# Moving the experts' gathers, the combination's split and the fold's product in a fused two-model kernel

## The chip, the cores and the metric

One core of a Trainium2 chip runs the whole program in one launch. The metric is device time in microseconds, the median of several executions. The engines are PE (TensorE: products, PEld its weight loads), DVE (VectorE), ACT (ScalarE), POOL (GpSimd) and SP (SyncE, which here only issues transfers).

## The reference, cut to what matters

Two small transformer stacks run one behind the other on 256 tokens of width 1024, in float32. The change lies in one stage, the second layer's feed-forward part with eight experts, of which each token uses two:

```python
def moe_swiglu(h, router_w, router_b, w1, w3, w2):      # h: 256 x 1024, w1 and w3: 8 x 1024 x 3584, w2: 8 x 3584 x 1024
    logits = (hf @ router_w) + router_b
    top_logit, top_idx = lax.top_k(logits, 2)
    top_w = jax.nn.softmax(top_logit, axis=-1)
    ...                                                  # rows of each expert in groups
    def expert_block(args):
        toks, e = args
        xb = h_pad[toks]
        return (jax.nn.silu(xb @ w1[e]) * (xb @ w3[e])) @ w2[e]
    ...
    y = y * row_w[:, None]
    out = jax.ops.segment_sum(y, row_tok, num_segments=T + 1)[:T]
```

So each expert takes the tokens that chose it (the gather), multiplies them by W1 and W3, then by W2, and its rows go back, weighted, to their tokens (the combination).

## The kernel before, in words

**Split products.** Each float32 operand is split into a high part in the type fp32r (a cast on ACT) and a low part (what is left, a subtraction on DVE), and a product is the sum of two or three products of parts. All weights are split so on their way: SP loads 1 MiB into a buffer `raw` (eight buffers in the experts' stage), ACT casts 1024 columns at a time into `whi`, DVE subtracts into `wlo`, and PE uses both.

**Places.** The eight experts are worked off in places 0 to 7, sorted by the number of their tokens. Even places hold up to 128 tokens. Odd places hold up to 64, and the 64 rows of the high part and the 64 of the low part lie side by side in one operand of 128 columns. So an even place needs three products for each block of weights and an odd one two, and then the two halves of the odd result have to be added: `folded` (line 1937) copies the bank `h` from PSUM to the buffer `hc` on ACT and multiplies it in plain float32 by a fixed matrix `fold` on PE, back into the same bank. There are 14 folds in an odd place: W1 and W3 of seven blocks of 512 columns.

**A place** has an up part (lines 2025 to 2050: seven blocks b, in each 8 x 512 columns of W1 and of W3) and a down part (lines 2053 to 2066: 28 steps of W2 into two banks `py`). In an odd place these are 224 and 112 products of 512 columns, in an even one 336 and 168.

**Chains.** Everything beside these products is written as Python generators. A list of chains is kept; behind each product of an odd place, and behind every first or second of an even one, `gap()` lets each chain go on to its next `yield`. A chain's step is held back while a rough model of the engines' times (`Meter`, `Flow`) says that its operands aren't ready. So the number of `yield`s sets how many products lie between two steps in PE's queue. The splits of the next weights are emitted between them by the same model. The chains that matter:

- `gather(e)` (line 1881), with `slots` (line 1812): compares positions to make a 0/1 matrix `oh` (DVE); for each half of the columns four products pick the rows (bank `m`), ACT scales them into `xt`, PE transposes, ACT adds a shift and casts the high part, DVE subtracts for the low part; at its end come `ct` and `ws` for the combination. It is started at the beginning of the down part of place e - 1 (line 2051) and has to be through before place e starts (line 2019). Even places use the first 128 columns of `src.hh` and `src.hl`, odd ones columns 128 to 256 of `src.hh`.
- `combine(e)` (line 1967): for each half, ACT scales `py` into `ys`, ACT casts it into `yh`, DVE subtracts into `yl`; then 16 products of `yh` and `yl` with `ct`, and DVE adds the result into `x`. It is started behind the place's last product, so that it runs in the next place's up part; for place 7 it is emitted at once.
- `hidden` and `hidden64` (lines 1919 and 1945): Silu, the product, transposes and the split of the inner activations; `hidden64` runs the fold first and waits for both.

Of the kernel before, what the change touches and what calls it, by code (L numbers as in the profile page):

```python
# [10 lines left out]
F32 = mybir.dt.float32  # L11
F32R = mybir.dt.float32r
I32 = mybir.dt.int32
AF = mybir.ActivationFunctionType
OP = mybir.AluOpType
PSUM = bass.MemoryType.PSUM

P = 128
T = 256
# [51 lines left out]
def shape_constants():  # L71

    i = np.arange(P)
    base, mix, moe, nsa = Pack(), Pack(), Pack(), Pack()
    base.add("ident", np.eye(P))
    base.add("ones", np.ones((P, P)))
# [312 lines left out]
class Kern:  # L389
# [1383 lines left out]
    def moe(self, src, sh, g, aim):  # L1773

        nc, tc = self.nc, self.tc
        from contextlib import ExitStack
        F = 3584
        with ExitStack() as es:
            pp = es.enter_context(tc.tile_pool(name="moe", bufs=2))
# [29 lines left out]
            X, C = {}, {}  # L1809
# [39 lines left out]
            def slots0(oh, xh, xl):  # L1849

                cs = pp.tile([P, 1], F32, name="cs")
                pc = self.nbank()
                ps = [psh.tile([P, 512], F32, name=f"h{q}") for q in range(2)]
                for q in range(2):
                    n = 0
                    for s in (th, tl):
                        for i in range(2):
                            nc.tensor.matmul(ps[q], oh[:, i], s[:, i, q * 512:(q + 1) * 512], start=(n == 0), stop=(n == 3))
                            n += 1
                    for i in range(2 if q == 0 else 0):  # L1860
                        nc.tensor.matmul(pc[:, :1], oh[:, i].bitcast(F32), src.y[:, i:i + 1], start=(i == 0), stop=(i == 1))
                nc.scalar.copy(cs, pc[:, :1])
                ts = [pp.tile([P, 512], F32, name=n, bufs=1) for n in ("xt", "ys")]
                pt = [psh.tile([P, 512], F32, name=f"h{q}") for q in range(2)]
                nc.scalar.mul(ts[0], ps[0], cs)
                nc.vector.tensor_scalar(ts[1], ps[1], cs, None, op0=OP.mult)
                for q in range(2):
                    for j in range(4):
                        nc.tensor.transpose(pt[q][:, j * P:(j + 1) * P], ts[q][:, j * P:(j + 1) * P], self.ident)
                ts = [t.rearrange("p (k s) -> p k s", k=4) for t in ts]  # L1870
                for q in range(2):
                    c = slice(4 * q, 4 * q + 4)
                    nc.vector.tensor_tensor(ts[q], pt[q].rearrange("p (k s) -> p k s", k=4),
                                            sh[:, c, None].to_broadcast([P, 4, P]), op=OP.add)
                    nc.scalar.copy(xh[:, c], ts[q])
                for q in range(2):
                    c = slice(4 * q, 4 * q + 4)
                    nc.vector.tensor_tensor(xl[:, c], ts[q], xh[:, c].bitcast(F32), op=OP.subtract)
                yield

            def gather(e):

                oh = pp.tile([P, 2, P], F32R, name="oh")
                while e and "wP" not in r:
                    yield
                pos = r["posP" if e else "pos"]
                for i in range(2):
                    nc.vector.tensor_scalar(oh[:, i], self.C("iota64" if e % 2 else "iota"), pos[:, i, e:e + 1], None,
                                            op0=OP.is_equal)
                for _ in range(9 if e else 1):  # L1890
                    yield
                if e % 2:
                    xh, xl = src.hh[:, :, P:P + 64], src.hh[:, :, P + 64:T]
                else:
                    xh, xl = src.hh[:, :, :P], src.hl[:, :, :P]
                if e == 0:
                    yield from slots0(oh, xh, xl)
                else:
                    yield from slots(e, oh, xh, xl)
                    yield  # L1900
                X[e] = (src.hh[:, :, P:T], None) if e % 2 else (xh, xl)
                if e == 0:
                    yield
                    while "w" not in r:
                        yield
                pt = misc()
                for i in range(2):
                    nc.tensor.transpose(pt[:, i * P:(i + 1) * P], oh[:, i].bitcast(F32), self.ident)
                for i in range(2):
                    nc.tensor.matmul(pt[:, 256:257], oh[:, i].bitcast(F32), r["wP" if e else "w"][:, i, e:e + 1],  # L1910
                                     start=(i == 0), stop=(i == 1))
                yield
                ct = pp.tile([P, T], F32R, name="ct")
                nc.scalar.copy(ct, pt[:, :T])
                ws = pp.tile([P, 1], F32, name="ws")
                nc.vector.tensor_copy(ws, pt[:, 256:257])
                C[e] = (ct, ws)

# [17 lines left out]

            def folded(h, done):

                c = pp.tile([P, 512], F32, name="hc", bufs=1)
                nc.scalar.copy(c, h)  # L1940
                yield
                nc.tensor.matmul(h[:64], self.C("fold"), c, start=True, stop=True)
                done.append(h)

# [22 lines left out]
            def combine(e, py, last):  # L1967
                ct, ws = C[e]
                yh = pp.tile([P, D], F32R, name="yh", bufs=1)
                yl = pp.tile([P, D], F32R, name="yl", bufs=1)  # L1970
                pts = []

                def spread(q):
                    pt = psh.tile([P, 512], F32, name=f"h{q % 2}") if last else misc()
                    for j in range(2):
                        kc = 2 * q + j
                        o = pt[:, j * T:(j + 1) * T]
                        nc.tensor.matmul(o, yh[:, kc * P:(kc + 1) * P], ct, start=True, stop=False)
                        nc.tensor.matmul(o, yl[:, kc * P:(kc + 1) * P], ct, start=False, stop=True)
                    pts.append(pt)  # L1980

                for q in range(2):
                    s = slice(q * 512, (q + 1) * 512)
                    y = pp.tile([P, 512], F32, name="ys", bufs=1)
                    nc.scalar.mul(y, py[q], ws)
                    yield
                    nc.scalar.copy(yh[:, s], y)
                    yield
                    nc.vector.tensor_tensor(yl[:, s], y, yh[:, s].bitcast(F32), op=OP.subtract)
                    yield  # L1990
                    if last:
                        spread(2 * q)
                        spread(2 * q + 1)
                for _ in range(1 if last else 9):
                    yield
                for q in range(4):
                    if not last:
                        spread(q)
                        yield
                    for j in range(2):  # L2000
                        kc = 2 * q + j
                        nc.vector.scalar_tensor_tensor(self.x[:, kc], pts[q][:, j * T:(j + 1) * T], g[:, kc:kc + 1],
                                                       self.x[:, kc], op0=OP.mult, op1=OP.add)
                        if last:
                            self.x_done(kc)
                    for _ in range(1 if last else 9):
                        yield

            gap = self.idle
            self.refill()  # L2010
            for b in self.ahead:
# [4 lines left out]
                next(first)  # L2016
            self.chain(first)
            for e in range(8):
                while any(c[2] == ("g", e) for c in self.chains):
                    self.rest()  # L2020
                xh, xl = X[e]
                few = e % 2 == 1
# [2 lines left out]
                for b in range(F // 512):  # L2025
                    hs, done = [], []
                    for w in range(2):
                        ps = psh.tile([P, 512], F32, name=f"h{w}")
                        k = 0
                        while k < KC:  # L2030
                            _, k0, nk, hi, lo = self.block()
                            assert k0 == k
                            for j in range(nk):
                                c = slice(j * 512, (j + 1) * 512)
# [13 lines left out]
                    else:  # L2048
                        self.wait_for(lambda n, ps, hs=hs, b=b: self.chain(hidden(hs[0], hs[1], b, ah, al)),
                                      b, None, always)  # L2050
                if e < 7:
                    self.chain(gather(e + 1), ("g", e + 1))
                py = [psy.tile([P, 512], F32, name="lin") for q in range(2)]
                for k in range(F // P):
                    _, k0, nk, hi, lo = self.block()
# [3 lines left out]
                    for q in range(2):  # L2059
                        c = slice(q * 512, (q + 1) * 512)  # L2060
# [14 lines left out]
                if e == 0:  # L2075
# [2 lines left out]
                    over = nc.values_load(r["over"][:1], min_val=0, max_val=1)  # L2078
                    with tc.If(over > 0):  # L2079
                        self.moe_rest(src, sh, r, th, tl, g, pp, p1, psh, misc)  # L2080
                self.chain(combine(e, py, False))
            self.extra = self.nbank = None

    def route(self, src, pool, misc):
# [1216 lines left out]
```

## Time and profile before

| | us |
|---|---|
| median of 3 runs | 3192.83 (3192.02 to 3202.15) |
| profiled execution | 3196.97 |
| its span | 3195.2 |
| PE busy in the span | 3040.6 (95%) |
| DVE busy | 2550.7 (80%) |
| ACT busy | 2029.0 (64%) |

The profile comes from one execution. It has a page with totals, a list of waits (who stood idle until whom), a chain of waits that leads back from the last instruction, a timeline, and windows, which give each engine's busy time in stretches that one chooses, with the mean clock that PE was granted (1.00 is 2.4 GHz), the busy share of the 16 transfer engines and their rate. A matmul's row is longer than the time to the next one, since they are pipelined: in a dense run of 512 columns a new one starts each 0.23 us and each row says about 0.40. All computing instructions bear the same line, that of a helper (L315), and are told apart by tile: `h` are the banks of the up part, `lin` those of the down part, `m` those of gather, transposes and combination.

### The profile page before, as it was taken

What the parts mean: (1) busy time and instruction counts of PE and PEld (TensorE: products, weight loads), DVE (VectorE), ACT (ScalarE), POOL (GpSimd) and SP (SyncE); (2) the same over time, 40 slices, a digit from 0 to 9 for tenths busy, and PEclk for the clock granted to TensorE, in tenths of its full rate; (3) what the DMA queues carried; (4) which work ended last, traced back from release to release, by engine and by line L of the source; (5) the groups of instructions that cost most, each with busy time, mean ns of one, the idle gap of its engine ahead of it and who ended that gap; (6) DMA issues with size and microseconds to landing.
All of it is one profiled execution on the core that took longest, in us unless ns stands there. A gap on an engine that the chain in (4) does not pass through costs nothing.

```text
span 3195.2 us, 55851 instructions
## 1 busy us (share of the span) xinstructions
PE 3040.6 (95%) x20747; PEld 2717.3 (85%) x20747; DVE 2550.7 (80%) x4692; ACT 2029.0 (64%) x3928; POOL 168.7 (5%) x551
## 2 busy tenths in 40 slices
PE   5999999999999998999999999999899999999999
PEld 5999999999999885686686686699888999998999
DVE  7787789867767888998998998898896666767775
ACT  5565555456665687887887877855675544555554
POOL 2322000003320000000000000000000000000000
PEclk9999999999999999999999999999999999999999
DMA  7334568842234798998999998744305554551354
GB/s 258 118 136 159 189 223 294 290 160 88 98 106 161 279 356 326 379 354 332 380 356 341 370 367 330 303 172 169 123 28 197 170 201 157 174 185 41 118 182 150
DMA packets 155354, 704.56 MB, mean 221 GB/s; under 512 B 15280, under 2 KB 19264, under 8 KB 111296
## 3 DMA queue, kind: packets, MB, share of 16 engines
q1 hardware_dynamic: 154176, 698.25, 60.4%
q8 instruction: 165, 2.70, 0.3%
q10 hardware_dynamic: 896, 2.65, 0.2%
q14 instruction: 117, 0.96, 0.1%
HBM read 699.76 MB, written 1.07 MB: 219 GB/s over the span
## 4 chain that ended last, share of the span: by engine, by line
PE 47%; ACT 6%; DVE 5%; issue 3%; DMA 1%; POOL 0%; ACTq 0%; SPq 0%; DVEq 0%; POOLq 0%
PE lin L315 29%; PE h L315 11%; ACT whi L315 3%; DVE wlo L315 2%; PE m L315 1%; PE o L315 1%; ACT hc L315 1%; PE b L315 1%; DVE wt L315 1%; PE c L315 1%; DVE w L315 1%; PE cmph L315 0%; PE a L315 0%; DVE s5Es L315 0%; PE more L315 0%
## 5 line engine op out<-in xcount | busy, mean ns | idle before, releaser
L315 ACT CAST whi<-raw 128x512 fp32r<-128x512 f32 (+4 forms) x1852 | 1329.2, 752 | 648.7 <-PE lin L315 328.7
L315 DVE TENSOR_TENSOR wlo<-raw,whi 128x512 fp32r<-128x512 f32 (+4 forms) x1852 | 1531.3, 856 | 244.2 <-ACT whi L315 226.0
L315 PE MATMUL lin<-hh,whi 128*128 128x256 f32 (+2 forms) x2968 | 866.8, 292 | 11.7 <-ACT whi L315 5.0
L315 PE MATMUL lin<-hh,wlo 128*128 128x256 f32 (+2 forms) x2968 | 855.3, 288 | 5.2 <-DVE wlo L315 5.1
L315 PE MATMUL lin<-hl,whi 128*128 128x256 f32 (+2 forms) x2968 | 852.7, 287 | 5.7 <-DVE hl L315 5.7
L315 PEld LDWEIGHTS lin<-hh,whi 128*128 128x128 f32 (+1 forms) x2968 | 566.9, 191 | 21.9 <-issue 5.8
L315 PEld LDWEIGHTS lin<-hh,wlo 128*128 128x128 f32 (+1 forms) x2968 | 566.6, 191 | 12.1 <-DVE wlo L315 7.5
L315 PEld LDWEIGHTS lin<-hl,whi 128*128 128x128 f32 (+1 forms) x2968 | 565.7, 191 | 8.8 <-DVE hl L315 6.6
L315 PE MATMUL h<-whi,hh 128*128 128x512 f32 x896 | 363.5, 406 | 6.1 <-PEq L2079 4.2
L315 PE MATMUL h<-wlo,hh 128*128 128x512 f32 x896 | 360.3, 402 | 3.7 <-DVE wlo L315 3.7
L315 PE MATMUL lin<-ah,wlo 128*128 128x256 f32 x928 | 262.0, 282 | 0.6 <-DVE wlo L315 0.6
L315 PE MATMUL lin<-al,whi 128*128 128x256 f32 x928 | 262.3, 283 | 0.0
L315 PE MATMUL lin<-ah,whi 128*128 128x256 f32 x928 | 262.1, 282 | 0.0
L315 PEld LDWEIGHTS h<-whi,hh 128*128 128x128 f32 x896 | 170.9, 191 | 86.6 <-issue 44.6
L315 PEld LDWEIGHTS h<-wlo,hh 128*128 128x128 f32 x896 | 170.8, 191 | 43.0 <-DVE wlo L315 6.8
L315 PE MATMUL lin<-wlo,mah 128*128 128x512 f32 x448 | 184.3, 411 | 5.7 <-DVE wlo L315 5.7
L315 PE MATMUL lin<-whi,mah 128*128 128x512 f32 x448 | 179.3, 400 | 0.1
L315 PEld LDWEIGHTS lin<-ah,wlo 128*128 128x128 f32 x928 | 175.5, 189 | 1.3 <-DVE wlo L315 1.3
L315 PE MATMUL h<-whi,hl 128*128 128x512 f32 x448 | 175.9, 393 | 0.2 <-DVE hl L315 0.2
L315 PEld LDWEIGHTS lin<-ah,whi 128*128 128x128 f32 x928 | 175.1, 189 | 0.0
L315 PEld LDWEIGHTS lin<-al,whi 128*128 128x128 f32 x928 | 175.0, 189 | 0.0
L315 DVE TENSOR_TENSOR f<-lin,rb 128x256 f32<-128x256 f32 (+1 forms) x232 | 97.8, 424 | 90.7 <-PE lin L315 89.7
(710 smaller groups left out, 4569.5 us busy)
## 6 DMA issues: line engine op xcount, KB each, us to landing
raw<-moe SPq DMA_DIRECT2D x336, 1024.0 KB, 6.9
raw<-b SPq DMA_DIRECT2D x88, 1024.0 KB, 4.9
raw<-win SPq DMA_DIRECT2D x60, 1024.0 KB, 4.9
adaraw<-ada SPq DMA_DIRECT2D x192, 256.0 KB, 5.3
raw<-b SPq DMA_DIRECT2D x64, 704.0 KB, 4.0
raw<-ffn SPq DMA_DIRECT2D x28, 1024.0 KB, 4.8
raw<-ffn SPq DMA_DIRECT2D x16, 896.0 KB, 4.7
raw<-updn SPq DMA_DIRECT2D x8, 1024.0 KB, 4.8
```

The lines of the kernel that those rows point to most:

```text
L315: return f(*args, **kw)
```

## The change

- Place 0 still starts gather 1 at its down part. The others go by a new chain `between`, started where the combination was: it runs the combination of place e, and for an even e then gathers e + 2 and e + 3. So gathers 2 and 3 run in place 1, 4 and 5 in place 3, 6 and 7 in place 5. Odd places alternate between `src.hh` and `src.hl` for their operand, and `ct` and `ws` get three buffers.
- In `combine` ACT scales PSUM straight into `yh`, and DVE computes `yl` from PSUM in one instruction. The buffer `ys` goes.
- `folded` lets three steps pass before the copy and six, not one, between copy and product.

```diff
--- before.py
+++ after.py
@@ -1860,7 +1860,7 @@
                     for i in range(2 if q == 0 else 0):
                         nc.tensor.matmul(pc[:, :1], oh[:, i].bitcast(F32), src.y[:, i:i + 1], start=(i == 0), stop=(i == 1))
                 nc.scalar.copy(cs, pc[:, :1])
-                ts = [pp.tile([P, 512], F32, name=n, bufs=1) for n in ("xt", "ys")]
+                ts = [pp.tile([P, 512], F32, name=n, bufs=1) for n in ("xt", "ms")]
                 pt = [psh.tile([P, 512], F32, name=f"h{q}") for q in range(2)]
                 nc.scalar.mul(ts[0], ps[0], cs)
                 nc.vector.tensor_scalar(ts[1], ps[1], cs, None, op0=OP.mult)
@@ -1890,7 +1890,8 @@
                 for _ in range(9 if e else 1):
                     yield
                 if e % 2:
-                    xh, xl = src.hh[:, :, P:P + 64], src.hh[:, :, P + 64:T]
+                    both = (src.hh, src.hl)[e // 2 % 2][:, :, P:T]
+                    xh, xl = both[:, :, :64], both[:, :, 64:]
                 else:
                     xh, xl = src.hh[:, :, :P], src.hl[:, :, :P]
                 if e == 0:
@@ -1898,7 +1899,7 @@
                 else:
                     yield from slots(e, oh, xh, xl)
                     yield
-                X[e] = (src.hh[:, :, P:T], None) if e % 2 else (xh, xl)
+                X[e] = (both, None) if e % 2 else (xh, xl)
                 if e == 0:
                     yield
                     while "w" not in r:
@@ -1910,9 +1911,9 @@
                     nc.tensor.matmul(pt[:, 256:257], oh[:, i].bitcast(F32), r["wP" if e else "w"][:, i, e:e + 1],
                                      start=(i == 0), stop=(i == 1))
                 yield
-                ct = pp.tile([P, T], F32R, name="ct")
+                ct = pp.tile([P, T], F32R, name="ct", bufs=3)
                 nc.scalar.copy(ct, pt[:, :T])
-                ws = pp.tile([P, 1], F32, name="ws")
+                ws = pp.tile([P, 1], F32, name="ws", bufs=3)
                 nc.vector.tensor_copy(ws, pt[:, 256:257])
                 C[e] = (ct, ws)
 
@@ -1936,9 +1937,12 @@
 
             def folded(h, done):
 
+                for _ in range(3):
+                    yield
                 c = pp.tile([P, 512], F32, name="hc", bufs=1)
                 nc.scalar.copy(c, h)
-                yield
+                for _ in range(6):
+                    yield
                 nc.tensor.matmul(h[:64], self.C("fold"), c, start=True, stop=True)
                 done.append(h)
 
@@ -1981,12 +1985,10 @@
 
                 for q in range(2):
                     s = slice(q * 512, (q + 1) * 512)
-                    y = pp.tile([P, 512], F32, name="ys", bufs=1)
-                    nc.scalar.mul(y, py[q], ws)
+                    nc.scalar.mul(yh[:, s], py[q], ws)
                     yield
-                    nc.scalar.copy(yh[:, s], y)
-                    yield
-                    nc.vector.tensor_tensor(yl[:, s], y, yh[:, s].bitcast(F32), op=OP.subtract)
+                    nc.vector.scalar_tensor_tensor(yl[:, s], py[q], ws, yh[:, s].bitcast(F32), op0=OP.mult,
+                                                   op1=OP.subtract)
                     yield
                     if last:
                         spread(2 * q)
@@ -2006,6 +2008,15 @@
                     for _ in range(1 if last else 9):
                         yield
 
+            def between(e, py):
+
+
+                yield from combine(e, py, False)
+                if e % 2 == 0:
+                    for n in (e + 2, e + 3):
+                        if n < 8:
+                            yield from gather(n)
+
             gap = self.idle
             self.refill()
             for b in self.ahead:
@@ -2016,7 +2027,7 @@
                 next(first)
             self.chain(first)
             for e in range(8):
-                while any(c[2] == ("g", e) for c in self.chains):
+                while e not in C and e > 0:
                     self.rest()
                 xh, xl = X[e]
                 few = e % 2 == 1
@@ -2048,8 +2059,8 @@
                     else:
                         self.wait_for(lambda n, ps, hs=hs, b=b: self.chain(hidden(hs[0], hs[1], b, ah, al)),
                                       b, None, always)
-                if e < 7:
-                    self.chain(gather(e + 1), ("g", e + 1))
+                if e == 0:
+                    self.chain(gather(1))
                 py = [psy.tile([P, 512], F32, name="lin") for q in range(2)]
                 for k in range(F // P):
                     _, k0, nk, hi, lo = self.block()
@@ -2078,7 +2089,7 @@
                     over = nc.values_load(r["over"][:1], min_val=0, max_val=1)
                     with tc.If(over > 0):
                         self.moe_rest(src, sh, r, th, tl, g, pp, p1, psh, misc)
-                self.chain(combine(e, py, False))
+                self.chain(between(e, py))
             self.extra = self.nbank = None
 
     def route(self, src, pool, misc):
```

## Rows read from the trace of the kernel before

**Rows 1.** The page: busy us, share of the span, instructions, by engine

```profile
PE 3040.6 (95%) x20747; PEld 2717.3 (85%) x20747; DVE 2550.7 (80%) x4692; ACT 2029.0 (64%) x3928; POOL 168.7 (5%) x551
```

**Rows 2.** Windows by part: us, busy PE PEld DVE ACT POOL, clock, DMA, GB/s

```profile
1208.20:1291.60 83.40, 75.54 (x291) 49.40 (x292) 72.98 (x77) 66.48 (x84) 0.00 (x0) 0.97 0.89 329
1291.60:1328.70 37.10, 34.67 (x145) 23.85 (x144) 33.94 (x35) 33.68 (x47) 0.00 (x0) 1.00 0.98 361
1328.70:1411.30 82.60, 82.57 (x378) 67.18 (x377) 79.16 (x81) 66.57 (x73) 0.00 (x0) 1.00 0.98 376
1411.30:1454.70 43.40, 43.40 (x199) 35.27 (x198) 35.81 (x36) 34.55 (x45) 0.00 (x0) 1.00 0.91 334
1454.70:1540.10 85.40, 76.31 (x291) 49.16 (x290) 74.17 (x78) 67.97 (x85) 0.00 (x0) 0.96 0.92 344
...
1703.30:1787.30 84.00, 74.91 (x291) 48.05 (x290) 73.88 (x78) 67.93 (x85) 0.00 (x0) 0.98 0.92 353
...
1950.50:2035.50 85.00, 75.90 (x292) 48.76 (x290) 74.13 (x78) 67.95 (x85) 0.00 (x0) 0.96 0.90 337
2035.50:2067.60 32.10, 31.60 (x119) 19.79 (x117) 31.30 (x31) 27.07 (x30) 0.00 (x0) 1.00 0.82 329
```

**Rows 3.** The chain of waits, experts' stage: start us, us, what

```profile
1358.80 11.10 PE h L315 x48
```

**Rows 4.** The list of waits, experts' stage: us in total, times, longest

```profile
PE h L315 <- ACT hc L315: 33.6, 56, 1.6
```

**Rows 5.** The timeline, a fold in place 7: start us, us, instruction, idle before

```profile
1978.53 0.39 PE L315 MATMUL h<-wlo,hh 128*128 128x512 f32 x1
...
1979.00 0.40 PE L315 MATMUL h<-wlo,hh 128*128 128x512 f32 x1
1979.26 0.57 ACT L315 COPY hc<-h 128x512 f32<-128x512 f32 x1
...
1979.89 1.07 PE L315 MATMUL h<-hc,c_moe 128*64 128x512 f32 x2 [0.49 <-ACT hc L315]
...
1980.89 0.50 PE L315 MATMUL h<-whi,hh 128*128 128x512 f32 x1
...
1981.23 0.39 PE L315 MATMUL h<-wlo,hh 128*128 128x512 f32 x1
```

**Rows 6.** The timeline, start of place 3

```profile
1456.34 0.62 ACT L315 CAST yh<-ys 128x512 fp32r<-128x512 f32 x1
...
1457.79 0.69 ACT L315 ACTIVATE ys<-lin,ws 128x512 f32<-128x512 f32 x1 [0.82 <-DVE yl L315]
...
1459.46 0.49 PE L315 MATMUL h<-whi,hh 128*128 128x512 f32 x1 [0.41 <-ACT whi L315]
1459.83 2.94 ACT L315 CAST whi<-raw 128x1024 fp32r<-128x1024 f32 x3
...
1460.72 0.50 PE L315 MATMUL h<-wlo,hh 128*128 128x512 f32 x1 [0.77 <-DVE wlo L315]
...
1462.67 0.58 ACT L315 COPY hc<-h 128x512 f32<-128x512 f32 x1
...
1463.30 1.97 PE L315 MATMUL h<-hc,c_moe 128*64 128x512 f32 x2 [1.61 <-ACT hc L315]
```

**Rows 7.** Windows, 5 us after that start (columns as in rows 2)

```profile
1465.00:1470.00 5.00, 5.00 (x15) 3.99 (x15) 2.95 (x4) 2.10 (x2) 0.00 (x0) 0.53 0.87 339
```

**Rows 8.** The timeline of DVE, end of place 3's down part

```profile
1572.93 8.04 DVE L315 TENSOR_TENSOR wlo<-raw,whi 128x1024 fp32r<-128x1024 f32 x7
```

**Rows 9.** The timeline of ACT, a gather in place 1's down part

```profile
1300.47 0.69 ACT L315 ACTIVATE xt<-m,cs 128x512 f32<-128x512 f32 x1 [0.40 <-PE m L315]
...
1303.89 1.14 ACT L315 ACTIVATE xt<-m,mod 128x128 f32<-128x128 f32 x4
```

**Rows 10.** The page's DMA issues: count, KB each, us to landing

```profile
raw<-moe SPq DMA_DIRECT2D x336, 1024.0 KB, 6.9
```

**Rows 11.** The list of waits of SP's queue, experts' stage

```profile
SPq L639 <- DVE wlo L315: 708.4, 296, 6.2
```

## Prediction

> **What bounds the kernel now.** I read the profile's page first: PE is busy for 95% of the span, DVE for 80%, ACT for 64% [rows 1], but such shares are means over stages, and the change touches one stage only, the eight experts, from about 1075 to 2072 us. So I cut that stage at the first product of each expert's up part (W1, W3) and down part (W2); one call for all those stretches shows what each engine did in each [rows 2]. Even and odd places differ. An even place's parts (82.6 and 43.4 us) have PE busy all the time: they are as long as their products, one per 0.231 us in a dense run [rows 3]. An odd place's up part takes 83.4 to 85.4 us although its 224 products need only 224 x 0.231 = 51.7 us; no engine is full in it (PE 76, DVE 74, ACT 68 of 85 us). So a wait is in it. The list of waits in the stage names it: PE's products waited 33.6 us for the copy hc, 56 times [rows 4]. The down part of place 1 holds a gather and takes 37.1 us (places 3 and 5 alike), that of place 7 holds none and takes 32.1; there DVE is nearly full (31.3 of 32.1).
>
> The timeline of one fold shows the wait itself [rows 5]. The last product of a half block starts at 1978.53, two products of the next follow, then PE stands until the copy (0.57 us, behind a cast) is done and starts the fold at 1979.89: 0.89 us after the product before it instead of 0.23, 0.66 us lost. The fold costs another 1.00 us of PE until 1980.89, and the product behind it 0.34 instead of 0.23: that stays. 14 folds a place lose 14 x 0.66 = 9.2 us.
>
> At the start of an odd place there is a second loss [rows 6]. The combination of the even place before it puts four instructions into ACT's queue; the second scaling waits 0.82 us for DVE's subtraction, since both halves use one buffer. The casts come late, then the first hc stands behind three casts in a row, and PE waits 1.61 us for it. The clock granted to PE then falls: 0.53 of full speed in the 5 us from 1465 [rows 7], nearly all of it at the lower of its two levels, 1.2 GHz, after the waits of rows 6. The fold that took 1.07 us takes 1.97.
>
> **The change part by part.**
>
> *Fold emitted later.* Three steps before the copy, six (was one) before the product; in an odd place a chain takes at most one step behind each product. Some nine products of 0.231 us (2.1 us) then lie between the last product and its fold, against 1979.89 - 1978.53 = 1.36 us for the chain of drain, copy and start. Of the 9.2 us a place all may go; at worst nothing, if the copy falls behind casts. I take all of it, for PE alone; what is late next comes below. Cover is the next half block's products. The banks of h are held some nine products longer out of the 32 of a block, and there are two of each: no wait.
>
> *Combination straight from PSUM.* Two casts of 0.62 us and ACT's wait of 0.82 us go, twice for eight places. DVE's step has the same 512 columns (yl, 0.69 us); with a PSUM operand and a scalar I bound it by -0.1 to +0.1 us each, since this form has no row at this size; I take the row's own 0.69, so 0 (the bounds are 1.6 us for all sixteen). In even places' up parts PE hides all of it (PE full, 82.57 of 82.6): nothing gained. In odd ones it is the hole of rows 6: 0.41 + 0.77 us for late casts, 1.0 us more than usual at the fold and about 3 us at the low clock, near 5 us in places 3 and 7, less in 5. At the end of place 7 nothing covers the combination, and there the second half starts 1.5 us earlier: -1.5.
>
> *Gathers 2 to 7 moved into odd places.* Two each in places 1, 3, 5, one behind the other, behind the combination. Gather 1 stays in place 0. SP and its transfers are not touched, and a gather issues no DMA. What each place gives back: an even down part (2, 4, 6) is 43.4 us for 168 products = 38.9 us; the remaining 4.5 us are 30 short instructions, 26 of them the gather's: -3.7 each, -11.1. PE is full there, so it all counts; I bound it by 3 and 4.5. An odd down part (1, 3, 5) falls to what place 7 shows without a gather: 37.1 - 32.1 = -5.0 each, -15.0 (4.5 to 5.5: 28 second halves of DVE at 8.04 / 7 = 1.15 us [rows 8] are 32.2 us and hold it there).
>
> What the odd up parts take on: two gathers, 2 x 3.7 us of PE, about 2 x 5 us of ACT (per half 0.69 us of scaling, 1.14 us for four additions [rows 9], and a cast like the 0.62 us of rows 6: 2.4 us or so, twice) and about 2 x 1.5 us of DVE. Sums for such an up part, from place 3's [rows 2, 6]: PE 85.4 - 9.2 for the folds - 5 for the hole at its start + 7.4 = 78.6 us; DVE 74.2 busy + 3 = 77.2; ACT 68.0 busy - 1.2 for two casts + 10 = 76.8. Three engines thus end within 2 us of each other: the room that the fold leaves is what the gathers use up. Below 78.6 it can't go; above, by as much as the three get in each other's way. Place 7's down part, as full on DVE, loses nothing to it; place 2's up part runs PE full with DVE at 79.2 of 82.6. I take 4 us of friction: 82.5 us instead of 83.4, 85.4, 84.0: -5.3 for the three (ends: 78.6, -17; and 90, +17, below). Place 7 has no gathers: PE 85.0 - 14.2 = 70.8, DVE 74.1; with the same 4 to 5 us I take 79 for 85.0, -6.0 (76 to 81.5).
>
> *Buffers.* ct and ws in three, ys gone: no time.
>
> *Sum:* -11.1 - 15.0 - 5.3 - 6.0 - 1.5 = -38.9 us. The profiled execution took 3196.97 us (span 3195.2), 4.1 above the median 3192.83; so 3158.1 for such an execution and about 3154 for the median.
>
> **Two rules against it.** The stage's 336 transfers of 1 MiB are 352.3 MB [rows 10]; place 2's up part drew 376 GB/s over 82.6 us, and the SP queue waited 708 us for buffers that DVE had not freed [rows 11], so the transfers have room. The Trainium skill (Perfetto Trace Analysis, Roofline) gives 358 GB/s as a core's share of the memory, and about 435 when one core is active. By the first the stage could end only about 8 us sooner; this trace goes beyond it, and by the second nothing would bind.
>
> ACT ran three casts ahead of the hc of rows 6 while PE waited 1.61 us. The Trainium skill (TensorE: Matmul & The Clock Gate, Architectural detail) says that ACT and DVE are strictly first in, first out. By that rule a copy emitted three steps later can fall behind more casts and the gathers' bursts; that is what the third rival prices.
>
> **Rivals.**
> 1. *The room isn't there.* Odd up parts become bound by ACT and DVE together: each gather costs 5.0 us as it did in the down parts, and only half of the fold's wait goes. For: the three sums above lie at the length of the part. Against: place 2's up part runs dense at 96% of DVE. Up parts with gathers 84.3 + 10.0 - 4.6 = 89.7, +16.2; place 7 -3.5; downs -26.1, end -1.5: -14.9, a median of about 3178.
> 2. *The transfers become the bound.* Odd places then draw 44.04 MB in 82.5 + 32.1 us, 384 GB/s, above every stretch of rows 2. If 355 GB/s (352.3 MB in 992 us), today's mean, is the limit, the stage keeps its length and only the end gains: 3191. Against: 376 seen, and SP's waits.
> 3. *Slower: ACT's order.* The copy waits behind bursts of 2.4 us in four spots of each up part with gathers, PE stands 1.6 us as at 1463.30, the clock falls, and each spot costs 5 us as in rows 6, beside the gathers' own 7.4, with no gain from the fold: 20 + 7.4 in three parts is +82 at the worst. It decides from 37.2 us for the three, 12.4 each, which is the gathers and one such spot a part: then the 27.6 us of the down parts and the end, and 9.6 more, are gone. With two spots, 17.4 each: +52.2 - 27.6 = +24.6, 3217. Against: the copy has 0.7 us of spare and gathers did not stop PE over 0.8 us in down parts.
> 4. *The fold doesn't move*, because the planner's readiness test already held it: up parts keep the wait and take 7.4 us each for gathers (+22), place 7 nothing: -5.4, 3187. Against: the steps are counted besides the test.
>
> **Chances.** Forecast 0.62; rival 1 0.18; rival 2 0.05; rival 3 0.08; rival 4 0.07. About 0.3% (9.6 us) is what a measurement of this kernel can tell from no change. Faster by more: forecast, rival 1 mostly: 0.79. Within: rivals 2 and 4 and a little of 1: 0.13. Slower: 0.08. The forecast's own range is 3140 to 3167 (up parts at 79.5 and 77, or at 85.5 and 81, and the bounds of the down parts); with rivals 1 and part of 4 it reaches 3184.
>
> **What would show it.** In the trace after: waits of PE on hc near 0; even down parts of 2, 4, 6 near 39.7; odd down parts near 32; odd up parts of 1, 3, 5 between 80 and 85 with ACT and DVE above 92%, that of 7 below 81; granted clock 1.00 at the start of odd places; even up parts unchanged at 82.6. It is wrong if the up parts with gathers pass 88 us, if PE's waits move to whi or wlo there by more than 5 us a part, or if ACT waits for PE in the gathers so that the first product of an even place comes late.

## The result, and the profile after

The changed kernel takes 3153.57 us (median of 4 runs, 3152.28 to 3156.13) where the kernel before takes 3192.43 (4 runs): the ratio is 0.9874, with a 95% interval of 0.986 to 0.9889 (it comes from all the runs, so it can differ in its last digits from the quotient of the medians). The profiled execution took 3156.13 us with a span of 3154.3. The forecast was 3154.

The windows of the changed kernel, by part as in [rows 2] (us, busy us and number of instructions of PE, PEld, DVE, ACT and POOL, granted clock, share and rate of the transfers): the parts of places 1 and 2, the up parts of 3 and 5, both parts of 7.

```profile
1209.80:1295.80 86.00, 84.31 (x342) 54.58 (x343) 76.10 (x85) 76.14 (x111) 0.00 (x0) 0.98 0.88 327
1295.80:1327.70 31.90, 31.63 (x120) 19.92 (x119) 31.82 (x32) 29.80 (x32) 0.00 (x0) 1.00 1.00 395
1327.70:1410.00 82.30, 82.30 (x377) 67.21 (x377) 79.22 (x81) 65.79 (x71) 0.00 (x0) 1.00 0.99 381
1410.00:1449.50 39.50, 39.50 (x173) 31.92 (x172) 35.33 (x31) 30.44 (x31) 0.00 (x0) 1.00 0.99 384
1449.50:1532.90 83.40, 82.52 (x343) 53.31 (x342) 76.91 (x87) 76.19 (x111) 0.00 (x0) 1.00 0.95 350
1686.50:1769.90 83.40, 82.55 (x344) 53.41 (x343) 76.98 (x87) 76.15 (x112) 0.00 (x0) 1.00 0.94 351
1923.50:1998.10 74.60, 74.13 (x292) 46.72 (x291) 73.87 (x78) 67.01 (x83) 0.00 (x0) 1.00 0.99 390
1998.10:2030.00 31.90, 31.62 (x119) 19.73 (x118) 30.84 (x31) 26.85 (x29) 0.00 (x0) 1.00 0.83 326
```

Place 1's down part has gone from 37.1 to 31.9 us, place 2's from 43.4 to 39.5. Place 7's up part has gone from 85.0 to 74.6, and PE is busy in it now, 74.13 of 74.60. The up parts with two gathers have hardly moved: 86.0, 83.4, 83.4 against 83.4, 85.4, 84.0. The clock that was 0.96 in place 3 is 1.00.

The view of the tile hc, its last part: what the instructions on it waited for, and who waited for it (us, times).

```profile
its engine sat idle before it (us, times) until:
  issue: 7.4, 22
  ACT whi L315: 7.3, 21
  ACT xt L315: 2.2, 6
who waited for it (us, times):
```

Behind the last line nothing follows: no wait for the copy is left where [rows 4] had 33.6 us. The three rows above it are other waits on the way to a fold, the longest of them for nothing that the profile shows (`issue`). The timeline of a fold in place 7 (start us, us, instruction), as in [rows 5]:

```profile
1962.31 0.58 ACT L315 COPY hc<-h 128x512 f32<-128x512 f32 x1
...
1963.47 0.40 PE L315 MATMUL h<-wlo,hl 128*128 128x512 f32 x1
...
1963.80 1.07 PE L315 MATMUL h<-hc,c_moe 128*64 128x512 f32 x2
...
1964.80 0.50 PE L315 MATMUL h<-whi,hl 128*128 128x512 f32 x1
```

The copy is through at 1962.89, the fold starts 0.9 us later, right behind the product before it (0.33 us, against 0.89).

The timeline of ACT at the start of place 3, as in [rows 6]:

```profile
1450.45 1.26 ACT L315 ACTIVATE yh<-lin,ws 128x512 fp32r<-128x512 f32 x2
1451.61 3.88 ACT L315 CAST whi<-raw 128x1024 fp32r<-128x1024 f32 x4
1455.39 0.58 ACT L315 COPY hc<-h 128x512 f32<-128x512 f32 x1
```

The two scalings come one behind the other, then four casts, then the first copy. That copy starts 5.9 us behind the part's start, 2.1 sooner than before (8.0), and its fold does not start until 1458.04, with products between. In the 5 us that answer to [rows 7], again 10.3 us behind the part's start, the clock is whole and PE full:

```profile
1459.80:1464.80 5.00, 5.00 (x22) 3.20 (x21) 5.00 (x6) 4.65 (x6) 0.00 (x0) 1.00 0.94 347
```

### The profile page after: what moved, and what is told of

The parts are those of the page before. It is cut to its first block, busy times and chain, and to the rows that moved or that the text cites. A ratio compares the mean times of both kernels' runs of the same rounds, so it can differ in the third digit from the quotient of the medians.

```text
span 3154.3 us, 55796 instructions
## 1 busy us (share of the span) xinstructions
PE 3037.1 (96%) x20747; PEld 2704.2 (86%) x20747; DVE 2551.2 (81%) x4692; ACT 2025.1 (64%) x3912; POOL 169.5 (5%) x551
## 3 DMA queue, kind: packets, MB, share of 16 engines
HBM read 699.76 MB, written 1.07 MB: 222 GB/s over the span
## 4 chain that ended last, share of the span: by engine, by line
PE 52%; DVE 7%; ACT 1%; issue 1%; DMA 1%; POOL 0%; SPq 0%; ACTq 0%; DVEq 0%; POOLq 0%
PE lin L315 30%; PE h L315 15%; DVE wlo L315 2%; PE m L315 2%; PE o L315 1%; DVE w L315 1%; DVE wt L315 1%; PE b L315 1%; PE cmph L315 1%; PE c L315 0%; DVE x L315 0%; ACT whi L315 0%; DVE s5Es L315 0%; PE x L315 0%; PE more L315 0%
## 5 line engine op out<-in xcount | busy, mean ns | idle before, releaser
L315 PE MATMUL h<-wlo,hh 128*128 128x512 f32 x672 | 272.3, 405 | 2.9 <-DVE wlo L315 2.8
L315 PE MATMUL h<-whi,hh 128*128 128x512 f32 x672 | 269.3, 401 | 4.9 <-ACTq L2090 4.3
L315 PE MATMUL h<-whi,hl 128*128 128x512 f32 x672 | 268.0, 399 | 0.3 <-DVE hl L315 0.3
L315 PEld LDWEIGHTS h<-whi,hh 128*128 128x128 f32 x672 | 127.2, 189 | 43.8 <-issue 13.0
L315 PEld LDWEIGHTS h<-wlo,hh 128*128 128x128 f32 x672 | 127.0, 189 | 43.5 <-DVE wlo L315 13.0
```

The source lines that it names most:

```text
L315: return f(*args, **kw)
```

## The experiments

All were timed against runs of the kernel before on their chip. The last two columns are the lengths of the up parts of places 3 and 7, in us, from one profiled execution of each kernel. In place 3 the folds, the hole at its start and the gathers meet; place 7 has no gathers.

| kernel | median us | before us | ratio, 95% interval | up part of place 3 | of place 7 |
|---|---|---|---|---|---|
| changed kernel | 3153.57 | 3192.43 | 0.9874 (0.986 to 0.9889) | 83.4 | 74.6 |
| fold alone | 3164.77 | 3194.68 | 0.9911 (0.9893 to 0.9929) | 76.4 | 76.4 |
| split alone | 3178.69 | 3194.68 | 0.9959 (0.9947 to 0.9971) | 80.1 | 80.2 |
| gathers alone | 3186.1 | 3194.68 | 0.9969 (0.9953 to 0.9984) | 89.7 | 82.5 |
| without fold | 3166.81 | 3194.68 | 0.9922 (0.9903 to 0.9942) | 84.5 | 80.2 |
| without split | 3169.61 | 3193.21 | 0.9919 (0.9898 to 0.994) | 85.2 | 76.3 |
| without gathers | 3154.1 | 3191.86 | 0.9884 (0.9868 to 0.9901) | 74.6 | 74.5 |
| changed, again | 3152.36 | 3191.86 | 0.9881 (0.9865 to 0.9898) | 83.4 | 74.5 |
| copy at once | 3150.86 | 3191.86 | 0.9878 (0.9861 to 0.9894) | 83.5 | 74.6 |
| one gather each | 3150.92 | 3191.86 | 0.9873 (0.9856 to 0.9889) | 79.2 | 74.6 |
| shift on DVE | 3163.95 | 3193.21 | 0.9908 (0.9889 to 0.9928) | 85.9 | 74.5 |
| gathers in even downs | 3153.94 | 3193.21 | 0.9876 (0.9856 to 0.9896) | 76.8 | 74.6 |
| no shift | 3148.94 | 3194.05 | 0.9871 (0.9852 to 0.9891) | 82.8 | 74.5 |

### Each part alone

**The fold alone.** The kernel before with the change's lines in `folded`:

```diff
+                for _ in range(3):
+                    yield
                 c = pp.tile([P, 512], F32, name="hc", bufs=1)
                 nc.scalar.copy(c, h)
-                yield
+                for _ in range(6):
+                    yield
```

> The kernel before with the fold's delays alone (three steps before the copy, six before the product). Theory (PE's wait for hc was the loss, 0.66 us in each of 56 folds): the waits on hc vanish, the odd up parts fall by about 9 us each, the down parts stay at 43.4 and 37.1, in all about -34 us, 3158. Rival (the up parts are bound by ACT and DVE as soon as the fold stops waiting, and the gathers' move is what pays): -10 us at most, 3182, with PE's waits on hc turned into waits on wlo.

Measured: -30 us, near the theory's -34. The odd up parts fell to 77.2, 76.4, 76.4 and 76.4, by 6 to 9 us; no wait for hc is left. Its window, place 3's up part:

```profile
1449.09:1525.47 76.38, 74.66 (x292) 46.73 (x291) 73.91 (x78) 68.29 (x86) 0.00 (x0) 1.00 0.96 376
```

The granted clock is 1.00 here too, although the combination still goes over ys: part of what was put down to the hole goes with the fold's wait.

**The split alone.** The kernel before with the change's lines in `combine`.

```diff
-                    nc.scalar.mul(y, py[q], ws)
-                    nc.scalar.copy(yh[:, s], y)
-                    nc.vector.tensor_tensor(yl[:, s], y, yh[:, s].bitcast(F32), op=OP.subtract)
+                    nc.scalar.mul(yh[:, s], py[q], ws)
+                    nc.vector.scalar_tensor_tensor(yl[:, s], py[q], ws, yh[:, s].bitcast(F32), op0=OP.mult,
+                                                   op1=OP.subtract)
```

> The kernel before with the combination straight from PSUM alone. Theory: the hole at the start of places 3, 5 and 7 shrinks by 3 to 5 us each and the granted clock stays at 1.00 there, the end of place 7 gains 1.5 us: about -12 us, 3180. Rival (the first fold behind the casts makes that hole, and ACT's shorter combination only moves it): the end alone, 3190, with the clock still near 0.5 in the 5 us behind the hole.

Measured: -16 us, where the theory had -12; the up parts of 3, 5 and 7 fell by 5.3, 3.9 and 4.8 us and their clock is 1.00. The theory holds. The waits for the copy stay; this is the list of waits in place 3's up part (us, times, longest), and the window of the 5 us in it that answer to [rows 7]:

```profile
PE h L315 <- ACT hc L315: 6.6, 12, 0.7
```

```profile
1464.20:1469.20 5.00, 4.52 (x20) 2.84 (x19) 5.00 (x6) 3.94 (x6) 0.00 (x0) 1.00 0.96 365
```

**The gathers' move alone.** The changed kernel with both other parts taken back.

> The kernel before with the gathers' move alone (and its third buffers of ct and ws). Theory: even down parts 39.5 instead of 43.4 and odd ones 31.9 instead of 37.1, -27 us in six parts, but the three odd up parts with two gathers take them on top of the fold's waits, +7 to +9 us each: in all about -4 us, 3188. Rival (the gathers' products go into the time that PE waits for the folds): odd up parts unchanged near 84.3, -27 us, 3165.

Measured: -8.6 us, near the theory's total but not by its parts. The down parts are what it says (39.5, 32.7), but two gathers lengthened the odd up parts by 4.1 to 4.5 us, not by 7 to 9, and PE's waits for hc fell from 33.6 to 19.6 us: by estimate about half of the gathers' products went into them. In this the truth lies between the two forecasts. The list of waits in the stage, and the first fold of place 7:

```profile
PE h L315 <- ACT hc L315: 19.6, 32, 1.6
```

```profile
1949.60 1.07 PE L315 MATMUL h<-hc,c_moe 128*64 128x512 f32 x2 [1.62 <-ACT hc L315]
```

Two changes that neither forecast names: the even up parts took 83.7 us, 1.2 more each (see the kernel without the split), and place 7's up part, which has no gathers in either kernel, took 82.5 instead of 85.0. PE's three waits at its start are as long as in the kernel before (0.41, 0.76 and 1.62 us against 0.41, 0.76 and 1.61), but the clock stayed at 1.00, and the fold took 1.07 us instead of 1.97. So, by estimate, the low clock cost place 7 of the kernel before some 2.5 us.

### Each part taken back

**Without the fold's delays.**

> The changed kernel with the fold's delays taken back. Theory: the waits on hc return in all four odd up parts; those with gathers take about 91 us and place 7's about 82, the down parts stay short: about +26 us on the changed kernel, 3180. Rival (the fold's delays add nothing once the combination is short and the gathers lie in the odd places): 3155.

Measured: 3166.8, +13 us on the changed kernel's 3153.6 on another chip (+11 when each is taken against the kernel before on its own chip), about half of the theory's 26. Place 7's part is 5.7 us longer than with them, those of 3 and 5, with gathers, only 1.1. Windows of places 3 and 7:

```profile
1448.58:1533.09 84.51, 81.44 (x343) 53.79 (x342) 76.43 (x87) 75.38 (x111) 0.00 (x0) 1.00 0.92 341
1926.55:2006.79 80.24, 73.12 (x291) 47.24 (x290) 73.72 (x78) 66.46 (x83) 0.00 (x0) 1.00 0.96 359
```

So where two gathers run, PE is nearly as busy without the delays (81.4 us) as with them (82.5): the fold's wait is filled by other products. The fold's delays and the gathers' move earn the same idle time.

**Without the gathers' move.**

> The changed kernel with the gathers back where they were (fold's delays and combination from PSUM alone). Theory: with the fold's waits gone a gather costs an odd up part 4.4 us, as place 7's 74.6 us against 83.4 in places 3 and 5 suggest, and the down parts it left cost 3.9 and 5.2 for theirs, so the move is worth next to nothing by now: all odd up parts near 75, down parts back at 43.4 and 37.1, 3151 to 3156. Rival (the move is worth what the down parts gave back): +25 us on the changed kernel, 3179.

Measured: 3154.1 against 3152.4 for the changed kernel beside it: no difference that these runs resolve. Windows of place 3:

```profile
1445.76:1520.33 74.57, 74.09 (x292) 46.67 (x291) 73.83 (x78) 66.95 (x84) 0.00 (x0) 1.00 0.98 388
1520.33:1556.82 36.49, 34.32 (x146) 24.00 (x145) 33.29 (x35) 33.46 (x46) 0.00 (x0) 1.00 0.98 371
```

The up part is 8.8 us shorter than with two gathers, the down part 4.6 us longer, and the even one, 43.4, 3.9 longer: 8.8 against 8.5. The theory holds, and it is the main finding: once the fold no longer waits, the move of the gathers is worth next to nothing, and the other two parts earn nearly all of the change's gain.

**Without the split.**

> The changed kernel with the combination over ys as before. Theory (the combination's detour on ACT delays casts for some 2 us at the start of each place; it shows where ACT and DVE bind, which is now the odd places alone): places 3, 5 and 7 longer by 2 us each, as the fold's delays alone had 76.4 us in their up parts against 74.6 with both, the end +1.5: +8 us, 3161, the granted clock 1.00. Rival (the hole of the kernel before comes back with its clock, 5 us a place): +16 us, 3169.

Measured: 3169.6, +16 us, the rival's total by another way. Places 3, 5 and 7 were 1.8 to 2.4 us longer, as the theory says. The clock was 1.00 in places 3 and 7, but in place 5 it fell to 0.75 for 5 us near the start, so there the rival has a part. The window of place 3's up part, and ACT at the start of place 2:

```profile
1451.74:1536.96 85.22, 83.12 (x344) 53.40 (x343) 76.97 (x86) 77.41 (x113) 0.00 (x0) 1.00 0.92 344
```

```profile
1333.11 0.69 ACT L315 ACTIVATE ys<-lin,ws 128x512 f32<-128x512 f32 x1 [2.12 <-PE h L315]
```

What neither forecast had is that the even up parts were longer too, 83.7 for 82.3: the second scaling into the shared buffer stood 2.1 us in front of ACT's next casts, which came late. In the kernel with the gathers' move alone it stood as long (2.13 us) and the parts took 83.7 as well; in the kernel before it stood 1.1 us and they took 82.6. So the gathers' move without the split costs 4.2 us there in three places. From place 7's down part on, the kernel took 1130 us for 1124. Of this 2.4 us are the end of place 7, which the theory put at 1.5; the rest lies in code that the edit does not touch, and what is behind place 7 varies from 1119.0 to 1124.5 us over the profiled executions of the other kernels.

### What a gather costs, and where

**The copy at once.** The three steps before the copy taken out of the changed kernel.

> The changed kernel without the three steps before the copy; the product stays six steps behind it. Theory (the distance between last product and fold is what counts: about seven products of 0.231 us are 1.6 us, more than the 1.36 us of drain, copy and start): no wait of PE on hc, 3154 within 2 us. Rival (a copy that comes at once stands at the head of ACT's queue until PE is through and holds back the casts behind it): ACT waits for PE 0.3 to 0.5 us at each of 56 copies, odd up parts 2 to 5 us longer, 3162 to 3174.

Measured: 3150.9, where the changed kernel beside it took 3152.4; the parts are as in that kernel (83.5, 74.6). The theory holds: the distance between last product and fold is what counts, and the first three steps are worth nothing.

**One gather in each odd up part.**

```diff
                 if e % 2 == 0:
-                    for n in (e + 2, e + 3):
-                        if n < 8:
-                            yield from gather(n)
+                    if e < 6:
+                        yield from gather(e + 2)
...
-                if e == 0:
-                    self.chain(gather(1))
+                if e % 2 == 0:
+                    self.chain(gather(e + 1))
```

> The changed kernel with one gather in each odd up part and one in each even down part: the gather of the next even place stays behind the combination, that of the next odd place goes back to the even place's down part. Theory (place 7's up part is as long as DVE needs, 73.9 of 74.6 us, and PE has some 3.5 us of room in it, so the first gather costs about 3 us and the second the rest of the 8.9): odd up parts of 1, 3, 5 near 77.5 to 78, even down parts 43.4, about -5 us on the changed kernel, 3148. Rival (each gather costs the same 4.4 us): 79 us, -1.5 us, 3152.

Measured: up parts of 80.7, 79.2 and 79.2 and 3150.9 us. The theory falls and the rival holds: there was no room for the first gather. It costs 4.6 us, the second 4.2. Its window (place 3's up part) shows PE just as full as in place 7:

```profile
1444.51:1523.68 79.17, 78.70 (x318) 49.80 (x317) 75.89 (x83) 71.69 (x98) 0.00 (x0) 1.00 0.95 364
```

**All in even down parts.** Gathers e + 1 and e + 2 start with the down part of an even place; only gather 2 stays behind a combination.

> The changed kernel with gathers 3 and 4 in place 2's down part, 5 and 6 in place 4's, 7 in place 6's, and only gather 2 behind a combination (place 1). Theory (a gather costs 3.9 us in an even down part, where PE alone is full and DVE and ACT have room, against 4.4 in an odd up part): even down parts 47.3, 47.3 and 43.4, odd up parts of 3 and 5 at 74.6, place 1's at 80.7: about -3 us on the changed kernel, 3150. Rival (two gathers don't end within 112 products, and the second runs on into the odd up part): that part near 77, no gain on the changed kernel.

Measured: the rival. The even down parts of places 2 and 4 took 45.2 us, and the second gather ran on into the odd up part, 76.8. With 3153.9 it is no better than the changed kernel. Place 3's up part:

```profile
1449.47:1526.23 76.76, 75.68 (x306) 48.59 (x305) 75.10 (x80) 69.91 (x91) 0.00 (x0) 1.00 0.96 372
```

**Is it ACT?** In place 3's up part of the changed kernel DVE stood 5.2 us for late casts:

```profile
DVE wlo L315 <- ACT whi L315: 5.2, 10, 0.8
```

Two kernels take work from ACT there. In the first the shift is added on DVE:

```diff
-                    for j in range(4):
-                        kc = 4 * q + j
-                        nc.scalar.activation(t[:, j], pt[:, j * P:(j + 1) * P], AF.Identity, bias=sh[:, kc:kc + 1])
+                    nc.vector.tensor_tensor(t, pt.rearrange("p (k s) -> p k s", k=4),
+                                            sh[:, 4 * q:4 * q + 4, None].to_broadcast([P, 4, P]), op=OP.add)
```

> The changed kernel with the gathers' four additions of the shift on ACT (1.14 us a half) replaced by one addition of 512 columns on DVE (about 0.6 us in a run). Theory (in the up parts with two gathers DVE is what binds, and beyond its own 77 us of work it stood 5.2 us in place 3 for casts that were late behind the gathers' bursts on ACT, against 0.7 us in place 7): DVE's waits for whi fall to 1 or 2 us, its own work grows by 2.4, the up parts take 81.5 to 82.5 us instead of 83.4, about -3 us in all. Rival (DVE alone binds and ACT's bursts cost nothing): the up parts take 85.5 to 86 us, +7 us.

Measured: 85.9 us in place 3, 87.4 in place 5, 3164 in all. The rival's number, but not its reason. The list of waits in place 3's up part:

```profile
ACT hh L315 <- DVE xt L315: 7.1, 4, 1.9
DVE wlo L315 <- ACT whi L315: 6.3, 8, 1.6
```

ACT now stood 7.1 us for DVE's addition, with the casts behind it, so this kernel does not decide. The second leaves the addition out:

```diff
-                    t = pp.tile([P, 4, P], F32, name="xt", bufs=1)
-                    for j in range(4):
...
+                    t = pt.rearrange("p (k s) -> p k s", k=4)
```

> The changed kernel with the addition of the shift left out of gathers 1 to 7 (the cast and the subtraction read PSUM), so that part of the computation is missing: it takes 1.14 us a half from ACT, two halves a gather, and gives nothing to another engine. Theory (the casts of the weights are late because they stand behind the gathers' bursts on ACT, and DVE, which binds, stands for them): the up parts of places 3 and 5 take 80 to 81 us instead of 83.4, DVE's waits for whi there fall from 5.2 us below 3. Rival (what a gather costs there is PE's and DVE's own work in turn with the planner's order, and ACT has the room): 83 us or more, waits unchanged.

Measured: 82.8 us in place 3, 82.7 in place 5, near the rival's 83 and not the theory's 80 to 81. Window and list of waits of that part:

```profile
1443.11:1525.90 82.79, 82.01 (x343) 53.47 (x343) 77.55 (x88) 71.59 (x96) 0.00 (x0) 1.00 0.96 355
```

```profile
DVE wlo L315 <- ACT whi L315: 4.3, 9, 1.5
```

ACT has 4.6 us less to do and the part is 0.6 us shorter. So ACT's bursts are not the main cost of a gather; PE's own work is. PE is busy for 82.0 of 82.8 us there, for 82.5 of 83.4 in the changed kernel, for 74.1 of 74.6 without gathers. A busy share can flatter PE, since its rows overlap, but the starts say the same. In place 3's up part without gathers only two instructions start more than 0.36 us behind the product of 512 columns ahead of them, and together they lose 0.9 us against the 0.23 us of a dense run; with two gathers six do, and lose 2.0 us. So of the 8.8 us that two gathers cost, by this estimate about 1.1 is standing and 7.7, or 3.9 a gather, is PE's work, as much as a gather costs in an even down part, where PE is full too. The 0.5 us a gather that is left no run here puts down to one engine.

Without gathers DVE is as full as PE (73.87 of 74.60 us in place 7), so that part does not tell the two apart. With gathers DVE is not: 76.91 of 83.40.

## Why the prediction was right

The total was right to within a microsecond, but two of its terms were off by about 5 us each and cancelled. That it came so near is luck; the mechanism of most terms was right. By the profiled executions, in us:

| term | forecast | measured |
|---|---|---|
| even down parts (2, 4, 6) | -11.1 | -11.8 |
| odd down parts (1, 3, 5) | -15.0 | -15.7 |
| odd up parts with two gathers | -5.3 | -0.1 |
| up part of place 7 | -6.0 | -10.5 |
| end of place 7 | -1.5 | -1.7 |
| even up parts (2, 4, 6) | 0 | -0.9 |
| before place 1's start; place 7's down part; behind the stage | 0 | +1.6; -0.2; -1.6 |
| sum | -38.9 | -40.9 |

*The wait in the odd up part* was read rightly. The fold alone is worth 30 us, and its up parts fell by 6 to 9 us where the step gave 9.2 a place. "Of the 9.2 us a place all may go" holds where nothing else fills the time: 5.6 us remain where the split is already in (80.2 to 74.6), 1.1 where two gathers run as well. The step also took the fold's loss 0.1 us too large: it counts 0.89 us against 0.23, but a fold that waits for nothing still starts 0.33 us behind the product before it. The parts alone add up to 54 us and together give 39: they share the same idle time, which the sum did not say.

*The hole at the start of odd places* was read rightly: near 5 us in place 3 (5.3), 5 in place 7 (4.8), less in 5 (3.9), and the clock came back. The low clock's part of it is some 2.5 us by place 7 of the gathers' move alone, where the forecast had about 3. But the fold alone brings the clock of place 3 back too, and so the hole and the folds are not two separate losses.

*The down parts* were measured where they were predicted, because the same part without a gather (place 7) and the dense run of an even place stood in the trace.

*The mis-sized term* is "PE 85.4 - 9.2 for the folds - 5 for the hole at its start + 7.4 = 78.6" with "4 us of friction". Place 7 shows what PE needs without gathers: 74.1 busy of 74.6, not 70.8, and next to no friction. There the fold alone takes off 8.7 us and the split alone 4.8, near the forecast's 9.2 and 5, but both together 10.5 and not 14.2: the sum counted some 3 us twice. In place 3 both together take off 10.8, and the two gathers cost 8.8 and not 7.4, which gives the measured 83.4. So the 4 us of friction in the forecast stood for a double count and for two gathers that were priced too low. In place 7 the same friction was added to DVE's 74.1, which made 79; it took 74.6. DVE's and ACT's sums for place 3, 77.2 and 76.8, are near the measured 76.9 and 76.2. Place 1, which PE began behind 4.3 us of standing and at the low clock, takes 86.0 (84.8 in the second profile). That and ACT's share in the three parts, 89 to 91%, lie at the edge of what the forecast's signs allowed (85 us and 92%).

*The rivals.* The first (ups at 89.7) did not come; its place 7, 81.5, neither. The second is ruled out: the odd down parts drew 395 GB/s, where [rows 2] had 361. That is above the 358 GB/s that the Trainium skill (Perfetto Trace Analysis, Roofline) gives as a core's share, and below its 435 for a lone core; the trace agrees with the second figure only. The third is ruled out too: the copy did fall behind casts, four of them at 1451.61, but the fold's distance covered it, and the kernel with the copy at once was as fast. In that row the trace agrees with the strict order that the Trainium skill gives for ACT and DVE (TensorE: Matmul & The Clock Gate, Architectural detail). The fourth did not come: the fold moved.

## What to carry to other kernels

Once a wait is removed, ask which engine is full in that stage before moving other work into it: here PE became full, and from then on each gather cost its own 4 to 5 us wherever it was put. Time the parts of a change alone and taken back, since two that fill the same idle time do not add, and one can cost time without another. A part of the same shape in the trace that lacks the work in question (place 7) prices a move better than a sum over engines.

## What the runs showed of the hardware

PE's clock fell in place 3 of the kernel before without a long gap: its waits there were 0.41, 0.77 and 1.61 us, with products between them. These waits alone do not settle it: with 0.41, 0.76 and 1.62 us at the start of place 7 the clock stayed at 1.00 in the kernel with the gathers' move alone, and fell to 0.73 and 0.59 in two stretches of 5 us in the kernel before. What made the difference no run here shows. The clock fell in both kernels at the start of place 1 too, where PE had stood for over 4 us at the branch behind place 0. In the changed kernel's window there products start 0.43 us apart from 1210.85 to 1213.84, and 0.23 apart again from 1214.11:

```profile
1210.00:1215.00 5.00, 5.00 (x15) 3.76 (x15) 1.64 (x2) 2.15 (x3) 0.00 (x0) 0.66 0.26 77
```

Behind a plain float32 fold the next weights are not loaded ahead. Their load starts with its own product, where in a dense run it starts 0.23 us before it, and PEld has stood 0.81 us for no releaser that the profile shows, before and after:

```profile
1964.80 0.19 PEld L315 LDWEIGHTS h<-whi,hl 128*128 128x128 f32 x1 [0.81 <-issue]
```

A scaling and subtraction in one instruction from PSUM costs DVE 0.74 us for 512 columns (median of 16), where the subtraction from SBUF took 0.69 (median of 16): 0.05 us more each, inside the bound of 0.1 that the forecast gave it.
